# A two-block kernel on one core: VectorE's side work tied behind the step it was written beside

## The chip, the core and the metric

The kernel runs on one core of a Trainium2 chip. A core has five engines that each work through a queue of their own in order: TensorE (PE: matrix multiplies, with its weight loads shown as PEld), VectorE (DVE), ScalarE (ACT), GpSimd (POOL) and SyncE (SP, which here only starts DMAs). The metric is the device time of the whole program in microseconds (us), as the median of several runs.

## The reference

Two transformer-like blocks run one after the other on 256 tokens of 2048 channels, all in float32. The first has an attention and an mLSTM mixer and then `peer`, a layer of 16,384 one-neuron experts, which is the part that changes. The second block (two attention layers) comes after it and is not changed.

```python
def peer(h, w_query, sub_keys_1, sub_keys_2, expert_down, expert_up):
    q = (h @ w_query).reshape(B, S, 8, 256)
    s1 = einsum('bshd,nd->bshn', q[..., :128], sub_keys_1)   # 128 scores
    s2 = einsum('bshd,nd->bshn', q[..., 128:], sub_keys_2)
    v1, i1 = top_k(s1, 16);  v2, i2 = top_k(s2, 16)
    vs, pos = top_k(v1[..., :, None] + v2[..., None, :], 16) # of 16 x 16
    idx = i1[pos // 16] * 128 + i2[pos % 16];  g = softmax(vs)
    a = gelu(einsum('td,thkd->thk', x, expert_down[idx]))
    return einsum('thk,thkd->td', g * a, expert_up[idx])
```

## The kernel before

Every float32 factor of a large product is split in two numbers of fewer bits, `hi` and `lo`, so that TensorE multiplies fast (helper `load`, lines 234 to 241): SP loads a piece `raw` of 128 x 1024 weights, ScalarE writes `hi` (line 239), VectorE writes `lo = raw - hi` (line 240), and then TensorE reads both (helper `mm3w`, lines 263 and 264). `wpools` says how many buffers of `raw`, `hi` and `lo` there are; the whole program has 4, 2 and 2, and a stage can add some for itself.

For 224 of the 256 tokens the expert layer is computed densely, for all experts, and the weights of those not picked are zero.

- **Search** (`topk`): products with `w_query` and the keys, then, on VectorE alone, the top 16 of 128 and of 256 for each of 8 heads and 2 halves of the tokens (`top16`: five instructions each), and the expert numbers (`eq`, `e`). It is a generator: each `yield` hands back to the loop that drives it. It leaves `eT`, the numbers and weights of the picked experts.
- **Down** (`down(n1)`, n1 = 0 to 127): 128 experts times 224 tokens into slot n1 of `R`, from two pieces of weights with eight pairs of matmuls each. At its end ScalarE copies half of the sum (line 308), VectorE adds the other half (line 309, `joined`), and ScalarE applies gelu (line 912). `R` is three tiles: slots 0 to 63, 64 to 95, 96 to 127.
- **Picks** (`picked`, 28 calls): VectorE makes one-hot tiles `o` (lines 874 and 879), TensorE multiplies them, ScalarE and VectorE bring the result to `gst` (lines 888 and 889), and GpSimd's queue stores it to DRAM as `gd`: the dense weights of 8 tokens.
- **Weigh** (`weigh`): GpSimd loads a piece of `gd` and multiplies it into `R` (line 900); 28 calls for the first tile of `R`, 28 for the other two.
- **Up**: two passes of 1024 channels. A step takes one slot of `R`, splits it into `w` (`split`: ScalarE line 312, VectorE line 313), loads one piece of weights, and runs 16 matmuls on eight accumulators.
- **Gathered rows** (`gathered`): the last 32 tokens are not in the dense part. Their rows of `expert_down` and `expert_up` are fetched by 64 indirect DMAs of 1 MB on GpSimd's queue (line 1026, two buffers), and VectorE uses each fetched tile once (a dot product at line 1036, a sum at line 1043).

The code says in which step a gathered row, a piece of the search or a pick stands. But the order of each engine's queue is made when the kernel is built, by a scheduler that puts an instruction in as soon as it reckons that its operands and buffers are there; `load` has a head start over its neighbours (`soon`). Nothing held the side work at the place in the code where it stood. On the chip each queue then runs strictly in that order.

Of the kernel before, what the change touches and what calls it, by code (L numbers as in the profile page):

```python
# [9 lines left out]
F32 = mybir.dt.float32  # L10
# [9 lines left out]
P = 128  # L20
S = 256
# [48 lines left out]
SD = 224  # L70
# [100 lines left out]
class K:  # L171
# [134 lines left out]
    def joined(self, out, ps):  # L306

        self.nc.scalar.copy(out, ps[:, 1, :])
        self.nc.vector.tensor_add(out, ps[:, 0, :], out)  # L309

    def split(self, hi, lo, src):
        self.nc.scalar.copy(hi, src)
        self.nc.vector.tensor_sub(lo, src, hi.bitcast(F32))  # L313

    def split_g(self, hi, lo, src, gain):

# [498 lines left out]
    def peer(self, x, r, xd, x2d):  # L815
# [4 lines left out]
        mm = nc.tensor.matmul  # L820
        ctx = ExitStack()
        hT = self.xt_tiles(self.pool(ctx, "ph", 1, "right"))
        wctx = ExitStack()
        self.wpools(wctx, 1, 2, 2, "right")
        sctx = ExitStack()
        sp = self.pool(sctx, "pr", 1, "right")
        some = sp.tile([P, NK, SG], F32, name="some")
# [17 lines left out]
        def slot(n1):  # L845
            i = 0 if n1 < 64 else 1 if n1 < 96 else 2
            return R[i][:, n1 - cuts[i], :]

        def more_R():
            i = len(R)  # L850
            n = cuts[i + 1] - cuts[i]
            R.append(self.pool(rctx, "R", 1).tile([P, n, SD], F32, name=f"R{i}"))

        ep = self.pool(wctx, "pe", 1, "right")
        eT = [ep.tile([P, S], F32, name=f"eT{i}") for i in range(2)] + [ep.tile([P, S, 2], F32, name="gT")]
        gd = self.dp.tile([P, P * SD], F32, name="gd")
        top, actx = ExitStack(), ExitStack()
        self.ada_open(actx, 3)
# [33 lines left out]
        def weigh(pool, which, t0):  # L892

            n0, n = cuts[which[0]], cuts[which[-1] + 1] - cuts[which[0]]
            st = pool.tile([P, 64, 8], F32, tag="gld", name=self.nm("gld"))[:, :n]
            o = t0 * P + n0 * 8
            nc.gpsimd.dma_start(st.rearrange("p n t -> p (n t)"), gd[:, o:o + n * 8])
            for i in which:
                d = R[i][:, :, t0:t0 + 8]
                nc.gpsimd.tensor_mul(d, d, st[:, cuts[i] - n0:cuts[i + 1] - n0, :])  # L900

        def down(n1):
            ps = self.ps([P, 2, SD], "mm")
            for s in range(2):
                hi, lo = self.load(a["down"], n1 * 2048 + s * 1024, 1024)
                for i in range(8):
                    c = s * 8 + i
                    w = slice(i * P, i * P + P)
                    self.mm3w(ps, hi[:, w], lo[:, w], hT[2][:, c, :, 0:SD], c == 0, c == NK - 1)
            r = slot(n1)  # L910
            self.joined(r, ps)
            nc.scalar.activation(r, r, AF.Gelu)  # L912

        for n1 in range(32):
            down(n1)
        n0 = 32
        for _ in search:
            down(n0)
            n0 += 1
        top.close()  # L920
        gctx = ExitStack()
        gp = self.pool(gctx, "pg", 2, "right")
        for n1 in range(n0, P):
            if n1 == 64:
                more_R()
            if n1 == 96:
                gctx.close()
                wctx.close()
                lp = self.pool(ctx, "pl", LAG1, "right")
                more_R()  # L930
            if n1 < 96:
                for i in range((n1 - n0) * (SD // 8) // (96 - n0), (n1 + 1 - n0) * (SD // 8) // (96 - n0)):
                    picked(i * 8)
            down(n1)
            if n1 >= 96 and n1 - 96 < SD // 8:
                weigh(lp, (0,), (n1 - 96) * 8)
        ctx.close()

        yctx = ExitStack()
# [9 lines left out]
        for i, (c0, c1) in enumerate(UP_PASSES):  # L949
            nb = (c1 - c0) // P  # L950
            acc = [self.ps([P, 2, SD], "at" if b < 4 else "mm") for b in range(nb)]
            for n1 in range(P):
                if i == 0 and n1 == 64:
                    lctx.close()
                hi, lo = self.load(a["up"], off, 1024)
                off += 1024
                w = up.tile([P, 2, SD], F32R, tag="w", name=self.nm("w"))
                self.split(w[:, 0, :], w[:, 1, :], slot(n1))
                for b in range(nb):
                    cs = slice(b * P, b * P + P)  # L960
                    self.mm3w(acc[b], hi[:, cs], lo[:, cs], w, n1 == 0, n1 == P - 1)
                if i == 0 and n1 % 2 == 1 and n1 // 2 < SD // 8:
                    weigh(lp, (1, 2), n1 // 2 * 8)
                k = i * P + n1
                if (k + 1) * 66 // 248 > k * 66 // 248:
                    next(rows, None)
            for b in range(nb):
                c = c0 // P + b
                g = self.av[:, 5, c:c + 1]
                nc.scalar.activation(yT[:, c, 0:SD], acc[b][:, 1, :], AF.Copy, scale=g)  # L970
                nc.vector.scalar_tensor_tensor(yT[:, c, 0:SD], acc[b][:, 0, :], g, yT[:, c, 0:SD], op0=OP.mult, op1=OP.add)
# [84 lines left out]
    def topk(self, tp, hT, eT, idd, gwd):  # L1056
# [22 lines left out]
        for h in range(8):  # L1079
            for t in range(2):  # L1080
                v = T("v", [2, 16], bufs=2)
                for half in range(2):
                    self.top16(tp, sc[:, h, t, half, :], P, v[:, half, :], idx[:, t, half, h, :])
                cand = T("cand", [16, 16], bufs=2)
                nc.vector.tensor_add(cand, v[:, 0, :].unsqueeze(2).to_broadcast([P, 16, 16]),
                                     v[:, 1, :].unsqueeze(1).to_broadcast([P, 16, 16]))
                self.top16(tp, cand.rearrange("p a b -> p (a b)"), 256, vs[:, t, h, :], pos[:, t, h, :])
        for t in range(2):
            ts = slice(t * P, t * P + P)
            fi = T("fi", [2, 8, 16])  # L1090
            nf = T("nf", [8, 16])
            nc.vector.tensor_copy(fi, idx[:, t])
            for half in range(2):
                pi = T("pi", [8, 16], U32)
                if half == 0:
                    nc.vector.tensor_single_scalar(pi, pos[:, t], 4, op=OP.logical_shift_right)
                else:
                    nc.vector.tensor_single_scalar(pi, pos[:, t], 15, op=OP.bitwise_and)
                pf = T("pf", [8, 16])
                nc.vector.tensor_copy(pf, pi)  # L1100
                eq = T("eq", [8, 16, 16])
                e = T("e", [8, 16])
                for h in range(8):
                    q = eq[:, h, :, :]
                    nc.vector.tensor_tensor(q, pf[:, h, :].unsqueeze(2).to_broadcast([P, 16, 16]),
                                            self.iota[:, 0:16].unsqueeze(1).to_broadcast([P, 16, 16]), op=OP.is_equal)
                    nc.vector.tensor_mul(q, q, fi[:, half, h, :].unsqueeze(1).to_broadcast([P, 16, 16]))
                nc.vector.tensor_reduce(e.rearrange("p a b -> p (a b)"), eq.rearrange("p a b c -> p (a b) c"),
                                        axis=AX.X, op=OP.add)
                if t == 1 and half == 0:  # L1110
                    nc.vector.tensor_scalar(nf, e, 128.0, None, op0=OP.mult)
                elif t == 1:
                    nc.vector.tensor_add(nf, nf, e)
                    nu = T("nu", [8, 16], U32)
                    nc.vector.tensor_copy(nu, nf)
                    nc.gpsimd.dma_start(idd, nu[P - SG:].rearrange("p a b -> p (a b)"))
                yield
                nc.vector.tensor_copy(eT[half][:, ts], self.to_eT(e))
            g = T("g", [8, 16])
            nc.vector.tensor_sub(g, vs[:, t], vs[:, t, :, 0:1].to_broadcast([P, 8, 16]))  # L1120
            nc.scalar.activation(g, g, AF.Exp)
            z = T("z", [8])
            nc.vector.tensor_reduce(z, g, axis=AX.X, op=OP.add)
            nc.vector.reciprocal(z, z)
            nc.vector.tensor_mul(g, g, z.unsqueeze(2).to_broadcast([P, 8, 16]))
            if t == 1:
                nc.gpsimd.dma_start(gwd, g[P - SG:].rearrange("p a b -> p (a b)"))
            yield
            ps = self.to_eT(g)
            hi = T("ghi", [P], F32R)  # L1130
            nc.scalar.copy(hi, ps)
            nc.vector.tensor_copy(eT[2][:, ts, 0], hi.bitcast(F32))
            nc.vector.tensor_sub(eT[2][:, ts, 1], ps, hi.bitcast(F32))
# [407 lines left out]
```

## Time and profile before

| what | value |
|---|---|
| median of three runs | 3271.24 us (3266.43 to 3271.97) |
| the profiled execution | 3278.16 us, its span 3276.0 us |
| PE, DVE, ACT, POOL busy, share of the span | 90%, 71%, 48%, 8% |
| mean granted TensorE clock, share of 2.4 GHz | 0.95 |

The page's slices show three places where TensorE's digit falls under 9 for long. Two are short (slices of 82 us each); the third is the first pass of up, where four slices in a row have a 5 and a clock digit of 7. The span is cut below at the first and last `joined` of the downs and at the end of the up passes: downs from 682 to 1444, up from 1444 to 2371. A window's row tells for each engine how long it was busy in it. A row of a timeline has the start, the duration, the engine, the line and the operation, and in square brackets how long the engine had been idle and who ended it.

### The profile page before, as it was taken

The page shows a single profiled execution, that of the slowest core. Times are in us where ns is not written, and L with a number is a line of the kernel's source. Part 1 is how long each engine was busy: PE and PEld are TensorE (multiplying, and loading weights), DVE is VectorE, ACT ScalarE, POOL GpSimd, SP SyncE. Part 2 cuts the span into 40 slices and gives each one's busy share as a digit, 9 for nine tenths or more (in the row PEclk, how much of TensorE's full clock was granted, in tenths as well). Part 3 has the DMA queues.
Part 4 walks back from the last instruction along what each step waited for, and adds up shares of the span by engine and source line. Part 5 has one row for each costly group of instructions (what it writes and reads, how often), then busy time and mean ns, then how long its engine had stood idle before and what let it go on. Part 6 is the DMA issues. An engine that isn't in the chain of part 4 may idle for free. (4 is left out here: it accounts for less than half of the span.)

```text
span 3276.0 us, 43208 instructions
## 1 busy us (share of the span) xinstructions
PE 2934.5 (90%) x15738; PEld 2540.2 (78%) x15738; DVE 2310.3 (71%) x3774; ACT 1586.6 (48%) x2585; POOL 277.3 (8%) x281
## 2 busy tenths in 40 slices
PE   6899998979999998985556899989999999999998
PEld 4577887868898887884445788878878888888887
DVE  7889976997788886556666555555568885566664
ACT  4455645424454544441212345545456665566663
POOL 0020000000000005227422000000000000000000
PEclk9899999989999999997777999999999999999999
DMA  9888885835566667678777665555653446545555
GB/s 400 322 314 318 327 296 192 331 122 190 180 209 214 216 214 230 224 235 292 280 276 276 209 198 188 195 181 197 198 178 126 136 151 219 183 165 168 167 167 167
DMA packets 182299, 724.86 MB, mean 221 GB/s; under 512 B 21367, under 2 KB 22435, under 8 KB 161059
## 3 DMA queue, kind: packets, MB, share of 16 engines
q1 hardware_dynamic: 152640, 604.70, 54.0%
q0 software_dynamic: 18640, 99.44, 8.2%
q10 hardware_dynamic: 10806, 17.95, 1.7%
q8 instruction: 124, 2.03, 0.3%
q14 instruction: 89, 0.73, 0.1%
HBM read 698.64 MB, written 23.38 MB: 220 GB/s over the span
## 5 line engine op out<-in xcount | busy, mean ns | idle before, releaser
L240 DVE TENSOR_TENSOR lo<-raw,hi 128x1024 fp32r<-128x1024 f32 x962 | 1182.3, 1232 | 668.9 <-ACT hi L239 662.8
L239 ACT CAST hi<-raw 128x1024 fp32r<-128x1024 f32 x962 | 993.1, 1042 | 1049.8 <-PE ps L263 630.9
L263 PE MATMUL ps<-xT,hi 128*128 128x448 f32 (+2 forms) x3104 | 1044.5, 388 | 25.6 <-ACT hi L239 20.6
L263 PE MATMUL ps<-w,hi 128*128 128x448 f32 x2048 | 727.6, 408 | 181.8 <-DVE w L313 173.4
L264 PE MATMUL ps<-xT,lo 128*128 128x224 f32 (+2 forms) x3104 | 852.8, 275 | 38.4 <-DVE lo L240 37.3
L263 PEld LDWEIGHTS ps<-xT,hi 128*128 128x128 f32 (+1 forms) x3104 | 590.2, 190 | 104.1 <-ACT hr L323 12.0
L264 PEld LDWEIGHTS ps<-xT,lo 128*128 128x128 f32 (+1 forms) x3104 | 596.8, 192 | 56.9 <-DVE lo L240 52.9
L263 PEld LDWEIGHTS ps<-w,hi 128*128 128x128 f32 x2048 | 416.0, 203 | 257.6 <-DVE w L313 218.2
L264 PE MATMUL ps<-w,lo 128*128 128x224 f32 x2048 | 566.8, 277 | 0.0
L255 PE MATMUL ps<-hi,xT 128*128 128x512 f32 x1152 | 462.9, 403 | 15.1 <-ACT xT L449 11.7
L256 PE MATMUL ps<-lo,xT 128*128 128x512 f32 x1152 | 462.7, 402 | 1.8 <-DVE lo L240 1.4
L257 PE MATMUL ps<-hi,xT 128*128 128x512 f32 x1152 | 462.6, 402 | 0.0
L264 PEld LDWEIGHTS ps<-w,lo 128*128 128x128 f32 x2048 | 423.3, 207 | 0.0
L255 PEld LDWEIGHTS ps<-hi,xT 128*128 128x128 f32 x1152 | 221.0, 192 | 65.4 <-ACT xT L449 13.1
L256 PEld LDWEIGHTS ps<-lo,xT 128*128 128x128 f32 x1152 | 221.2, 192 | 51.9 <-DVE lo L240 4.2
L257 PEld LDWEIGHTS ps<-hi,xT 128*128 128x128 f32 x1152 | 220.3, 191 | 49.5 <-DVE xT L450 0.7
L379 DVE CUSTOM_DVE_ANT_0 aw<-aw,sB 128x2048 f32<-128x2048 f32 x96 | 220.0, 2306 | 27.5 <-ACT sB L366 19.0
L912 ACT ACTIVATE R<-R 128x224 f32<-128x224 f32 x128 | 50.1, 392 | 331.5 <-DVE R L309 331.5
L1036 DVE CUSTOM_DVE_ANT_0 rows<-rows,hB 128x2048 f32<-128x2048 f32 x32 | 73.8, 2307 | 66.7 <-DMA rows<-in_down_rows_dram,gidx 66.7
L1043 DVE SCALAR_TENSOR_TENSOR gacc<-rows,gdot,gacc 128x2048 f32<-128x2048 f32 x31 | 72.9, 2351 | 57.7 <-DMA rows<-in_up_rows_dram,gidx 57.7
L313 DVE TENSOR_TENSOR w<-R,w 128x224 fp32r<-128x224 f32 x256 | 106.5, 416 | 0.0
L900 POOL TENSOR_TENSOR R<-R,gld 128x256 f32<-128x256 f32 (+1 forms) x84 | 97.7, 1181 | 36.2 <-DMA gld<-gd 35.6
(398 smaller groups left out, 2479.1 us busy)
## 6 DMA issues: line engine op xcount, KB each, us to landing
raw<-in_down_dram SPq DMA_DIRECT2D x256, 512.0 KB, 3.5
raw<-in_up_dram SPq DMA_DIRECT2D x256, 512.0 KB, 3.3
aw<-in_w_ada_dram SPq DMA_DIRECT2D x96, 1024.0 KB, 7.7
raw<-in_b_in_dram SPq DMA_DIRECT2D x128, 512.0 KB, 3.3
raw<-in_w_in_dram SPq DMA_DIRECT2D x112, 512.0 KB, 6.1
raw<-in_a_in_dram SPq DMA_DIRECT2D x49, 512.0 KB, 3.2
raw<-in_w_out_dram SPq DMA_DIRECT2D x32, 512.0 KB, 4.0
raw<-in_w_query_dram SPq DMA_DIRECT2D x32, 512.0 KB, 7.2
```

The source lines that it names most:

```text
L239: self.nc.scalar.copy(hi[:, :n], raw)
L240: self.nc.vector.tensor_sub(lo[:, :n], raw, hi[:, :n].bitcast(F32))
L255: mm(out, lh, rh, start=start, stop=False)
L256: mm(out, lh, rl, start=False, stop=False)
L257: mm(out, ll, rh, start=False, stop=stop)
L263: mm(out, wh, x, start=start, stop=False)
L264: mm(out[:, 0, :], wl, x[:, 0, :], start=False, stop=stop)
L313: self.nc.vector.tensor_sub(lo, src, hi.bitcast(F32))
L379: nc.vector.tensor_tensor_reduce(out=w, in0=w, in1=self.sB, scale=1.0, scalar=0.0, op0=OP.mult, op1=OP.add, accum_out=out)
L900: nc.gpsimd.tensor_mul(d, d, st[:, cuts[i] - n0:cuts[i + 1] - n0, :])
L1036: nc.vector.tensor_tensor_reduce(out=t, in0=t, in1=h, scale=1.0, scalar=0.0, op0=OP.mult, op1=OP.add, accum_out=dj)
L1043: nc.vector.scalar_tensor_tensor(acc, t, dj, acc, op0=OP.mult, op1=OP.add)
```

## The change

`joined` and `split` return their VectorE instruction. The blocks that drive the search, the picks and the gathered rows are put under `tc.issue_after(...)` of it: each VectorE instruction of such a block comes later in VectorE's queue than the instruction named. It is an order in one queue; instructions of other engines in the block are not held. The search has more `yield`s and is driven one or two pieces per down from down 0 on. The picks run to row 112. Buffers: the stage up to the end of the search adds one of `raw`, `hi` and `lo` each (before: 1, 2 and 2, until row 96), so it has 3 of `hi` and `lo`, and the downs after it have 2 (before: 4). From up step 64 on there is a third `hi`. The pools of `eT` and of the picks are opened earlier.

```diff
     def joined(self, out, ps):
         self.nc.scalar.copy(out, ps[:, 1, :])
-        self.nc.vector.tensor_add(out, ps[:, 0, :], out)
+        return self.nc.vector.tensor_add(out, ps[:, 0, :], out).ins
...
+        ep = self.pool(ctx, "pe", 1, "right")
+        eT = ...
+        gp = self.pool(ctx, "pg", 2, "right")
         wctx = ExitStack()
-        self.wpools(wctx, 1, 2, 2, "right")
+        self.wpools(wctx, 1, 1, 1, "right")
...
-        for n1 in range(32):
-            down(n1)
-        n0 = 32
-        for _ in search:
-            down(n0)
+        n0, end = 0, object()
+        more = True
+        while more:
+            with tc.issue_after(down(n0)):
+                for _ in range(1 + n0 % 2):
+                    more = more and next(search, end) is not end
             n0 += 1
         top.close()
-        gctx = ExitStack()
-        gp = self.pool(gctx, "pg", 2, "right")
+        wctx.close()
+        n2 = 112
         for n1 in range(n0, P):
...
-            if n1 < 96:
-                for i in range((n1 - n0) * (SD // 8) // (96 - n0), ...):
-                    picked(i * 8)
-            down(n1)
-            if n1 >= 96 and n1 - 96 < SD // 8:
-                weigh(lp, (0,), (n1 - 96) * 8)
+            with tc.issue_after(down(n1)):
+                for i in range((n1 - n0) * (SD // 8) // (n2 - n0), ...):
+                    if n1 < n2:
+                        picked(i * 8)
+            if n1 >= 100:
+                weigh(lp, (0,), (n1 - 100) * 8)
...
                 if i == 0 and n1 == 64:
                     lctx.close()
+                    self.wpools(ctx, 0, 1, 0, "right")
...
-                self.split(w[:, 0, :], w[:, 1, :], slot(n1))
+                last = self.split(w[:, 0, :], w[:, 1, :], slot(n1))
...
                 if (k + 1) * 66 // 248 > k * 66 // 248:
-                    next(rows, None)
+                    with tc.issue_after(last):
+                        next(rows, None)
```

In the up passes VectorE's queue before, at steps 23 to 25 of the first pass: a gathered row (`rows`, `gdot`) stands in every step, one `lo` and one `w` between two of them.

```order
L1036 ISA rows_15172,gdot<-rows_15172,hB 128x2048
L1036 ISA gdot 128x1
L240 TENSOR_TENSOR lo_13899<-raw_13896,hi_13898 128x1024
L313 TENSOR_TENSOR w_13902<-R_5422,w_13902 128x224
L1036 ISA rows_15275,gdot<-rows_15275,hB 128x2048
```

And now, at steps 18 to 22 (the lines' numbers have moved by some, 1036 is 1041):

```order
L1041 ISA rows_13646,gdot<-rows_13646,hB 128x2048
L1041 ISA gdot 128x1
L240 TENSOR_TENSOR lo_13734<-raw_13731,hi_13733 128x1024
L313 TENSOR_TENSOR w_13737<-R_5425,w_13737 128x224
L240 TENSOR_TENSOR lo_13763<-raw_13760,hi_13762 128x1024
L313 TENSOR_TENSOR w_13766<-R_5425,w_13766 128x224
L240 TENSOR_TENSOR lo_13788<-raw_13785,hi_13787 128x1024
L313 TENSOR_TENSOR w_13791<-R_5425,w_13791 128x224
L240 TENSOR_TENSOR lo_13817<-raw_13814,hi_13816 128x1024
L313 TENSOR_TENSOR w_13820<-R_5425,w_13820 128x224
L1041 ISA rows_13728,gdot<-rows_13728,hB 128x2048
```

Three or four steps stand between two gathered rows. Before, the 64 of them stood behind steps 5 to 62 of 256; now they stand behind steps 5 to 241, each right behind a `w`.

GpSimd's queue in the first pass now, with three multiplications of the second half of `R` (`R_9238` and `R_11282`, weighed by `gld`) around the fifth gather:

```order
L898 DMA gld_14200<-gd 128x512
L1031 DMA rows_13646<-in_down_rows_dram,gidx 128x2048
L901 TENSOR_TENSOR R_9238<-R_9238,gld_14143 128x32x8
L901 TENSOR_TENSOR R_11282<-R_11282,gld_14143 128x32x8
L901 TENSOR_TENSOR R_9238<-R_9238,gld_14200 128x32x8
L901 TENSOR_TENSOR R_11282<-R_11282,gld_14200 128x32x8
```

Before, one gather stood behind every two loads of `gld` at most. Now the fourth, the fifth and the sixth gather have 5, 10 and 10 loads of `gld`, with some two multiplications each, between them and the gather ahead.

VectorE's queue at a pick before (`o` and `gst` are the pick's tiles; at the end of down `ps_7780` the `lo` of two more downs, `ps_7864` and `ps_7912`, have been written: the last are `lo_7916` and `lo_7938`):

```order
L240 TENSOR_TENSOR lo_7916<-raw_7913,hi_7915 128x1024
L874 TENSOR_TENSOR o_7961<-cst,eT_4530 128x512
L240 TENSOR_TENSOR lo_7938<-raw_7935,hi_7937 128x1024
L309 TENSOR_TENSOR R_5422<-ps_7780,R_5422 128x224
L889 TENSOR_TENSOR gst_7828<-ps_7836,gst_7828 128x128x2
L889 TENSOR_TENSOR gst_7828<-ps_7841,gst_7828 128x128x2
L889 TENSOR_TENSOR gst_7828<-ps_7853,gst_7828 128x128x2
L889 TENSOR_TENSOR gst_7828<-ps_7858,gst_7828 128x128x2
L879 SCALAR_TENSOR_TENSOR o_7963<-cst,eT_4529,gT 128x256 x4
L874 TENSOR_TENSOR o_7978<-cst,eT_4530 128x512
L879 SCALAR_TENSOR_TENSOR o_7980<-cst,eT_4529,gT 128x256
L240 TENSOR_TENSOR lo_8000<-raw_7997,hi_7999 128x1024
```

And now (874, 879, 889 are 875, 880, 890; at the end of down `ps_9151` the `lo` of one more down, `ps_9239`, have been written; `lo_9291` and `lo_9313` are for the down behind that):

```order
L309 TENSOR_TENSOR R_5425<-ps_9151,R_5425 128x224
L875 TENSOR_TENSOR o_9200<-cst,eT_4390 128x512
L880 SCALAR_TENSOR_TENSOR o_9202<-cst,eT_4389,gT 128x256 x4
L875 TENSOR_TENSOR o_9217<-cst,eT_4390 128x512
L890 TENSOR_TENSOR gst_9199<-ps_9207,gst_9199 128x128x2
L880 SCALAR_TENSOR_TENSOR o_9219<-cst,eT_4389,gT 128x256 x2
L240 TENSOR_TENSOR lo_9291<-raw_9288,hi_9290 128x1024
L890 TENSOR_TENSOR gst_9199<-ps_9212,gst_9199 128x128x2
L880 SCALAR_TENSOR_TENSOR o_9219<-cst,eT_4389,gT 128x256 x2
L890 TENSOR_TENSOR gst_9199<-ps_9224,gst_9199 128x128x2
L890 TENSOR_TENSOR gst_9199<-ps_9229,gst_9199 128x128x2
L240 TENSOR_TENSOR lo_9313<-raw_9310,hi_9312 128x1024
```

A pick is now whole within one down: its results are added (`gst`) in the same down in which its one-hot tiles are made, so VectorE's queue goes through TensorE and ScalarE and back between two `lo`. Nine of its instructions stand between the end of a down and the first `lo` behind it, and the store of `lo` reaches one down less far ahead than before.

## Rows read from the trace of the kernel before

**Rows 1.** Windows: from, to, length, busy time (count) per engine, granted clock, DMA share, GB/s.

```profile
682.00:969.00 287.00, 254.43 (x1502) 235.28 (x1503) 229.67 (x542) 130.18 (x212) 3.19 (x6) 0.95 0.54 175
...
1444.00:1845.00 401.00, 241.43 (x1085) 212.86 (x1086) 257.63 (x233) 89.41 (x136) 169.96 (x153) 0.77 0.77 275
...
2010.00:2371.00 361.00, 344.63 (x2070) 312.31 (x2068) 204.82 (x292) 175.42 (x269) 0.99 (x2) 0.98 0.59 192
```

**Rows 2.** Waits, window 1444:1845: who waited for whom, us, times, longest.

```profile
PE ps L263 <- DVE w L313: 161.4, 49, 10.4
```

**Rows 3.** Groups by line: names, shapes, count | busy us, mean ns | idle before, releasers.

```profile
L1036 DVE CUSTOM_DVE_ANT_0 rows<-rows,hB 128x2048 f32<-128x2048 f32 x32 | 73.8, 2307 | 66.7 <-DMA rows<-in_down_rows_dram,gidx 66.7
...
L1043 DVE SCALAR_TENSOR_TENSOR gacc<-rows,gdot,gacc 128x2048 f32<-128x2048 f32 x31 | 72.9, 2351 | 57.7 <-DMA rows<-in_up_rows_dram,gidx 57.7
```

**Rows 4.** Timeline of VectorE, 1616:1622: start, us, engine, line, names [idle before].

```profile
1616.59 2.29 DVE L1036 CUSTOM_DVE_ANT_0 rows<-rows,hB 128x2048 f32<-128x2048 f32 x1 [3.12 <-DMA rows<-in_down_rows_dram,gidx]
...
1618.81 1.22 DVE L240 TENSOR_TENSOR lo<-raw,hi 128x1024 fp32r<-128x1024 f32 x1
...
1619.94 0.38 DVE L313 TENSOR_TENSOR w<-R,w 128x224 fp32r<-128x224 f32 x1
```

**Rows 5.** Timeline, 1902:1910, an up step with no gathered row.

```profile
1902.06 1.05 ACT L239 CAST hi<-raw 128x1024 fp32r<-128x1024 f32 x1 [1.53 <-PE ps L263]
...
1907.43 1.05 ACT L239 CAST hi<-raw 128x1024 fp32r<-128x1024 f32 x1 [1.53 <-PE ps L263]
...
1908.51 1.23 DVE L240 TENSOR_TENSOR lo<-raw,hi 128x1024 fp32r<-128x1024 f32 x1 [1.33 <-ACT hi L239]
...
1909.65 0.38 DVE L313 TENSOR_TENSOR w<-R,w 128x224 fp32r<-128x224 f32 x1
```

**Rows 6.** Timeline of VectorE, ends of six downs, the first and last among them.

```profile
682.15 0.40 DVE L309 TENSOR_TENSOR R<-ps,R 128x224 f32<-128x224 f32 x1
...
836.90 0.38 DVE L309 TENSOR_TENSOR R<-ps,R 128x224 f32<-128x224 f32 x1
...
841.92 0.38 DVE L309 TENSOR_TENSOR R<-ps,R 128x224 f32<-128x224 f32 x1
...
964.64 0.38 DVE L309 TENSOR_TENSOR R<-ps,R 128x224 f32<-128x224 f32 x1
...
976.97 0.39 DVE L309 TENSOR_TENSOR R<-ps,R 128x224 f32<-128x224 f32 x1
...
1443.84 0.38 DVE L309 TENSOR_TENSOR R<-ps,R 128x224 f32<-128x224 f32 x1
```

**Rows 7.** Groups by line: VectorE's search and picks.

```profile
L1051 DVE FIND_INDEX8 idx<-v,sc 128x8 uint32<-128x128 f32 x32 | 9.5, 296 | 0.0
...
L1051 DVE FIND_INDEX8 pos<-vs,cand 128x8 uint32<-128x256 f32 x16 | 6.9, 429 | 0.0
...
L1105 DVE TENSOR_TENSOR eq<-pf,cst 128x256 f32<-128x256 f32 x32 | 12.3, 415 | 0.0
...
L874 DVE TENSOR_TENSOR o<-cst,eT 128x512 fp32r<-128x512 f32 x56 | 38.4, 685 | 0.1
...
L879 DVE SCALAR_TENSOR_TENSOR o<-cst,eT,gT 128x256 fp32r<-128x256 f32 x224 | 95.6, 479 | 0.0
...
L889 DVE TENSOR_TENSOR gst<-ps,gst 128x256 f32<-128x256 f32 x112 | 39.9, 421 | 0.0
```

**Rows 8.** Windows of line 240 alone: VectorE busy (count), granted clock, DMA share, GB/s.

```profile
1300.00:1320.00 20.00, 12.28 (x7) 1.00 0.82 266
...
1380.00:1400.00 20.00, 9.37 (x8) 1.00 0.64 207
```

**Rows 9.** Timeline of GpSimd, 1480:1502: weights multiplied into R.

```profile
1486.97 2.83 POOL L900 TENSOR_TENSOR R<-R,gld 128x256 f32<-128x256 f32 x4 [1.63 <-DMA gld<-gd]
...
1493.72 3.04 POOL L900 TENSOR_TENSOR R<-R,gld 128x256 f32<-128x256 f32 x4
```

**Rows 10.** Tile rows: the gathers' DMAs.

```profile
DMA to landing us min/median/max: 5.4/7.1/10.2
```

More of the change, by code (lines that the diff above doesn't have):

```diff
@@ L308, in joined @@
         self.nc.scalar.copy(out, ps[:, 1, :])
-        self.nc.vector.tensor_add(out, ps[:, 0, :], out)
+        return self.nc.vector.tensor_add(out, ps[:, 0, :], out).ins
     def split(self, hi, lo, src):
         self.nc.scalar.copy(hi, src)
-        self.nc.vector.tensor_sub(lo, src, hi.bitcast(F32))
+        return self.nc.vector.tensor_sub(lo, src, hi.bitcast(F32)).ins
     def split_g(self, hi, lo, src, gain):
@@ L822, in peer @@
         hT = self.xt_tiles(self.pool(ctx, "ph", 1, "right"))
+        ep = self.pool(ctx, "pe", 1, "right")
+        eT = [ep.tile([P, S], F32, name=f"eT{i}") for i in range(2)] + [ep.tile([P, S, 2], F32, name="gT")]
+        gp = self.pool(ctx, "pg", 2, "right")
         wctx = ExitStack()
-        self.wpools(wctx, 1, 2, 2, "right")
+        self.wpools(wctx, 1, 1, 1, "right")
         sctx = ExitStack()
@@ L852, in more_R @@
             R.append(self.pool(rctx, "R", 1).tile([P, n, SD], F32, name=f"R{i}"))
-        ep = self.pool(wctx, "pe", 1, "right")
-        eT = [ep.tile([P, S], F32, name=f"eT{i}") for i in range(2)] + [ep.tile([P, S, 2], F32, name="gT")]
         gd = self.dp.tile([P, P * SD], F32, name="gd")
@@ L910, in down @@
             r = slot(n1)
-            self.joined(r, ps)
+            last = self.joined(r, ps)
             nc.scalar.activation(r, r, AF.Gelu)
-        for n1 in range(32):
-            down(n1)
-        n0 = 32
-        for _ in search:
-            down(n0)
+            return last
+        n0, end = 0, object()
[4 more added lines that the diff above has]
+                    more = more and next(search, end) is not end
             n0 += 1
         top.close()
-        gctx = ExitStack()
-        gp = self.pool(gctx, "pg", 2, "right")
+        wctx.close()
+        n2 = 112
         for n1 in range(n0, P):
@@ L926, in peer @@
             if n1 == 96:
-                gctx.close()
-                wctx.close()
+                more_R()
+            if n1 == 100:
                 lp = self.pool(ctx, "pl", LAG1, "right")
-                more_R()
-            if n1 < 96:
-                for i in range((n1 - n0) * (SD // 8) // (96 - n0), (n1 + 1 - n0) * (SD // 8) // (96 - n0)):
-                    picked(i * 8)
-            down(n1)
-            if n1 >= 96 and n1 - 96 < SD // 8:
-                weigh(lp, (0,), (n1 - 96) * 8)
+            with tc.issue_after(down(n1)):
+                for i in range((n1 - n0) * (SD // 8) // (n2 - n0), (n1 + 1 - n0) * (SD // 8) // (n2 - n0)):
+                    if n1 < n2:
+                        picked(i * 8)
+            if n1 >= 100:
+                weigh(lp, (0,), (n1 - 100) * 8)
         ctx.close()
@@ L1083, in topk @@
                     self.top16(tp, sc[:, h, t, half, :], P, v[:, half, :], idx[:, t, half, h, :])
+                    yield
                 cand = T("cand", [16, 16], bufs=2)
@@ L1087, in topk @@
                 self.top16(tp, cand.rearrange("p a b -> p (a b)"), 256, vs[:, t, h, :], pos[:, t, h, :])
+                yield
         for t in range(2):
@@ L1107, in topk @@
                     nc.vector.tensor_mul(q, q, fi[:, half, h, :].unsqueeze(1).to_broadcast([P, 16, 16]))
+                    if h % 2:
+                        yield
                 nc.vector.tensor_reduce(e.rearrange("p a b -> p (a b)"), eq.rearrange("p a b c -> p (a b) c"),
```

## The prediction

> **What bounds the kernel now.** I read the page's slices first, then the windows, the waits of the worst window, the groups by line, and the timelines of a slow and a clean step. TensorE is the engine to keep fed: it is busy 90% of the span. The windows show where it isn't. From 1444 to 1845, in the first pass of up, it is busy for 241 of 401 us, at a granted clock of 0.77, so part of the time at the lower of its two levels (1.2 and 2.4 GHz); in the second pass (2010 to 2371) it is busy for 345 of 361 at 0.98 [rows 1]. In the slow window TensorE waits for VectorE's `w`: 161 us in 49 waits [rows 2]. VectorE isn't short of time there (258 of 401 busy); it stands at the head of its own queue and waits for gathered rows: 66.7 and 57.7 us [rows 3]. The timeline shows how: a row waits 3.1 us for its DMA, takes 2.3, and only then come the `lo` and `w` that TensorE needs [rows 4].
>
> The downs from 682.2 to 1443.8 [rows 6] have a second loss. At 837 a down takes 5.01 us, which for 16 pairs of matmuls is TensorE's own pace; 128 of them would be 641 us, and they take 762. One part is the search, which the scheduler poured into VectorE's queue in one piece around 682 to 760; from 682 to 969 VectorE is busy 230 of 287 us and the clock is 0.95 [rows 1]. Another is the picks: two downs with a pick take 12.33 us instead of 10.03 [rows 6].
>
> **The search, spread.** Its VectorE instructions stay the same in number: five per top-16, 32 sets like the first row and 16 sets like the second (five and a sum), 5 x 9.5 + 6 x 6.9 = 89 us [rows 7]. Over the 32 downs that now carry them that is 2.8 us per down, beside 2 x 1.23 for `lo` and 0.38 for line 309, 5.6 by the rows; back to back they overlap by some 0.09 each (the `w` of [rows 4] starts 1.13 us after a `lo` of 1.22), which leaves about 4.9, just under TensorE's 5.01. The `lo` run a piece ahead with 3 buffers, so I take 32 x 5.01 = 160 us, hidden behind TensorE. The rest, 64 `eq` instructions (2 x 12.3 us [rows 7]) with as much again in sums and small ones (an estimate), is some 3 us per down over 15 downs: 5.5 us each, VectorE being now the slower, 83 us. If the cover fails, the cost is at most the whole of it, 89 + 44 us.
>
> **The picks.** They get dearer. The downs behind the search lose two `hi` and two `lo` buffers. With two, the `lo` of a down's second half can't be made before the half two back is done: `hi` 1.05, `lo` 1.23 against a half of 2.5 us. Now a pick stands in front of it. From the end of a down at 0: `hi` to 1.05, `lo` to 2.3, line 309 to 2.6, the first one-hot tiles (0.69 and 0.48 each [rows 7]) from 2.6 to 4.9. TensorE reaches the pick's first matmul in its queue at 1.9 and gets its operands at 3.7; the last of four at 4.9, so its first half ends at 5.3 instead of 2.5. The second half needs the other tiles, behind a `gst` addition that waits for ScalarE: 6.3 for the third pair of pick matmuls' first, and, since a `lo` of 1.23 stands in between, 8.6 for the last; it ends at 9.75. A down with a pick so takes 9.75, one without 5.04 to 5.2. 28 x 9.75 + 52 x 5.1 = 538 us. Bounds: as in the row of before, 12.33 - 5.01 = 7.3 per pick down (69 us less); fully in series, TensorE's 6 us, the pick's 6.2 ((38.4 + 95.6 + 39.9) / 28) and a `hi`, `lo` and `w`, 2.6: 14.8 (141 us more). I take my walk, as it follows the new queues.
>
> **Weighing beside picks.** 28 multiplications of GpSimd now run while VectorE is pressed. A `lo` took 1.75 us (12.28 / 7) in a window with them and 1.17 without [rows 8]. I charge 10 us in the downs and 5 in up. In the same rows the granted clock is 1.00, so it isn't TensorE's. The Trainium skill, page "SBUF — State Buffer", section "SBUF: two separate sides", says that VectorE with two inputs in SBUF and a GpSimd operation that reads SBUF shut each other out for a whole instruction; the trace shows a slowing by half, not a wait of the whole; by the rule the charge is 82 us, a rival below.
>
> **Downs:** 160 + 83 + 538 + 10 = 791 us, 29 more than the 762 of before.
>
> **Up, base.** Two clean steps take 5.37 us (1902.06 to 1907.43): with two buffers, ScalarE's `hi`, VectorE's `lo` and `w` follow each other [rows 5]. 64 steps x 2.68 = 172. From step 64 on there is a third `hi`, so `lo` starts as soon as its own buffer is free: 1.23 + 0.38 us against a step's 8 pairs of 2.51. 192 x 2.51 = 482 us. If the third buffer doesn't help: 33 more.
>
> **Up, gathered rows.** 64 x 2.33 us on VectorE [rows 3]. In the first 64 steps a row holds `lo` back by 1.3 us behind a step whose slack is nothing; the next step, which would have waited 0.35, doesn't: 1.0 each, 17 us for 17. Later only the part beyond the slack is late, 0.6 each, 28 us for 47. The DMA wait goes: a gather is issued when the row two before it is used, 7.5 steps or 19 us ahead, and lands in 7.1 (10.2 at most) [rows 10]. Two gathers fall out: GpSimd's queue puts ten weighings ahead of the fifth and ten more ahead of the sixth. Two weighings and a gather took 6.75 us (1486.97 to 1493.72 [rows 9]), so ten without gathers some 27. By that the fifth lands some 13 us after VectorE wants it and the sixth some 18 after, and VectorE stands in front of all `lo`: 33 us with TensorE's restart. Between 0 (if the weighing were far quicker) and 50. The very first row waits in both kernels: 4. What the second pass has beyond 128 x 2.68 = 343 of its 361 us [rows 1], the change of passes and the positions' block, stays: 18.
>
> **Up:** 172 + 482 + 17 + 28 + 33 + 4 + 18 + 5 = 759, against 2371 - 1444 = 927. A gain of 168.
>
> **Sum.** 168 - 29 = 139 us less than the profiled execution's 3278: 3139. The runs' median lies 7 us below that execution, so I forecast 3132. All queues behind up read as before, so nothing is won or lost there.
>
> **Rivals.**
>
> - *The ties put engines in series* (slower). Place: downs 0 to 112. VectorE's tied piece starts only behind line 309, which waits for TensorE; TensorE waits for the `lo` behind the piece. If nothing overlaps, the search costs its whole 133 us where the forecast has 8, 125 more, and the picks take 14.8 per down, 141 more: 3398. It decides from somewhat over half of these 266 us, where the 139 are eaten. For it: fewer buffers, and the pick's way through three engines and back. Against: with 3 buffers `lo` is a piece ahead in the search.
> - *The gathers still wait for their DMAs* as they did, 124 us in sum [rows 3]: about 3240. For it: the indirect DMA goes through a queue full of weighings. Against: 38 of the 64 come after the weighings, with 19 us of lead.
> - *All hidden.* A pick costs as before and GpSimd's queue is no brake: 69 + 33 less, 3030.
> - *The lock.* Each weighing shuts VectorE out for its whole length: 56 x 0.73 us (3.0 / 4 [rows 9]) and 28 of twice that, 82 instead of 15: 3199.
>
> **How the numbers follow.** Forecast 0.60, all hidden 0.12, lock 0.12, DMA waits 0.07, series 0.09. The forecast's own bounds (33 for the third buffer, 50 and 0 for the two gathers, 69 of the picks) give 3060 to 3200. The range goes from 3055 to 3220, which leaves out the series, the DMA waits and the far end of all hidden. Faster by over 0.2% (about what a measurement here can tell from no change): 0.89, within it 0.03, slower 0.08, which is the series where it goes past the middle.
>
> **What would show it.** Right: TensorE waits on `w` of a few tens of us instead of 161; up 760 us long with two single waits of 10 to 20 us for a gathered row within its first 120 us; downs longer than before, with some 4 us of TensorE's waiting for `o` and `lo` at each pick; no stretch in which VectorE is full at the downs' start. Wrong: downs as short as before or shorter, up steps of 2.7 us to the end, or DVE waiting for a row's DMA through both passes.

## The result and the profile after

The changed kernel takes 3175.86 us (median of four runs, 3173.10 to 3177.91) against 3271.60 for the kernel before in the same comparison: a ratio of 0.9705, interval 0.9686 to 0.9725. That is 96 us faster, inside the forecast's range and on its side, but 44 us short of the 3132 that was forecast. The profiled execution took 3177.91 us, its span 3176.2.

Cut at the same instructions, the two profiled executions (spans 3276.0 and 3176.2) compare like this:

| stretch, us | before | after | change | forecast change |
|---|---|---|---|---|
| start to the first `joined` of the downs | 671.7 | 668.7 | -3 | 0 |
| first to last `joined` | 772.1 | 825.2 | +53 | +29 |
| last `joined` to the last `w` of up | 919.8 | 767.9 | -152 | -168 |
| from there to the end | 912.4 | 914.4 | +2 | 0 |

One row has to be put right first. The end of a down at 682.15 in [rows 6] is the second, not the first. The first stands here, in VectorE's timeline of the kernel before:

```profile
671.74 0.39 DVE L309 TENSOR_TENSOR R<-ps,R 128x224 f32<-128x224 f32 x1
```

So the downs of before took 772 us from the first end to the last. These are 127 downs, as many as the forecast adds up (32, 15 and 80); the 762 that it set against them are for one less.

The page's slices of the changed kernel (busy tenths, 79 us each): where the first pass of up had 5, 5, 5 and 6 for TensorE, a 6 and a 7 are left in slices 20 and 21; the row of 8s from slice 13 to 18, in the downs, is new.

```profile
PE   6899998999998888889678999989999999999998
```

The windows of the changed kernel, cut at its own steps (columns as in [rows 1]): the downs with the search, the downs with picks, the first 64 steps of up, and the rest of up.

```profile
668.73:843.22 174.49, 166.25 (x1037) 154.59 (x1036) 168.60 (x498) 82.72 (x129) 0.00 (x0) 1.00 0.58 191
...
926.76:1415.99 489.23, 408.27 (x2312) 361.44 (x2311) 359.16 (x591) 217.16 (x373) 69.19 (x82) 0.94 0.55 184
...
1494.19:1737.74 243.55, 180.45 (x1019) 163.19 (x1020) 143.17 (x162) 84.95 (x128) 95.57 (x107) 0.88 0.70 247
1737.74:2261.80 524.06, 494.05 (x3056) 458.58 (x3056) 405.94 (x482) 258.92 (x397) 75.72 (x48) 0.99 0.80 286
```

The loss in the downs sits in the second row: TensorE works 408 of 489 us there, at a granted clock of 0.94. What is left of the old loss in up sits in the third: 180 of 244 us, clock 0.88.

In the waits from 1494 to 1845, TensorE's wait for `w` answers to [rows 2], 69 us for 161, and the second row is new in kind: three waits, of which one lasts 18.9 us.

```profile
PE ps L263 <- DVE w L313: 69.0, 33, 19.4
...
DVE rows L1041 <- DMA rows<-in_down_rows_dram,gidx: 37.2, 3, 18.9
```

The groups of gathered rows answer to [rows 3]: the work is the same, of 124 us of waiting 37 are left, all of it in the first half.

```profile
L1041 DVE CUSTOM_DVE_ANT_0 rows<-rows,hB 128x2048 f32<-128x2048 f32 x32 | 73.7, 2302 | 37.2 <-DMA rows<-in_down_rows_dram,gidx 37.2
L1048 DVE SCALAR_TENSOR_TENSOR gacc<-rows,gdot,gacc 128x2048 f32<-128x2048 f32 x31 | 72.7, 2345 | 0.0
```

In the later part of the first pass, VectorE's `w` come like this (1753.67 to 1764 has four steps). A step without a row takes 2.51 us, the one behind a row is late, and the steps behind it catch up part of it:

```profile
1753.67 0.39 DVE L313 TENSOR_TENSOR w<-R,w 128x224 fp32r<-128x224 f32 x1
...
1756.18 0.39 DVE L313 TENSOR_TENSOR w<-R,w 128x224 fp32r<-128x224 f32 x1
1756.48 2.29 DVE L1041 CUSTOM_DVE_ANT_0 rows<-rows,hB 128x2048 f32<-128x2048 f32 x1
...
1759.83 0.39 DVE L313 TENSOR_TENSOR w<-R,w 128x224 fp32r<-128x224 f32 x1
...
1761.27 0.39 DVE L313 TENSOR_TENSOR w<-R,w 128x224 fp32r<-128x224 f32 x1
...
1764.34 0.39 DVE L313 TENSOR_TENSOR w<-R,w 128x224 fp32r<-128x224 f32 x1
```

### The profile page after: what moved, and what is told of

Same layout as the page of the kernel before. It is cut to its first block, busy times and chain, and to the rows that moved or that the text cites. A ratio compares the mean times of both kernels' runs of the same rounds, so it can differ in the third digit from the quotient of the medians.

```text
span 3176.2 us, 43138 instructions
## 1 busy us (share of the span) xinstructions
PE 2888.3 (91%) x15738; PEld 2504.3 (79%) x15738; DVE 2336.5 (74%) x3774; ACT 1605.2 (51%) x2585; POOL 279.8 (9%) x281
## 5 line engine op out<-in xcount | busy, mean ns | idle before, releaser
L263 PE MATMUL ps<-xT,hi 128*128 128x448 f32 (+2 forms) x3104 | 1056.2, 389 | 16.2 <-ACT hi L239 10.5
L263 PE MATMUL ps<-w,hi 128*128 128x448 f32 x2048 | 669.5, 384 | 95.6 <-DVE w L313 92.9
L264 PE MATMUL ps<-w,lo 128*128 128x224 f32 x2048 | 546.7, 267 | 0.0
L263 PEld LDWEIGHTS ps<-w,hi 128*128 128x128 f32 x2048 | 391.4, 191 | 148.8 <-DVE w L313 113.3
L264 PEld LDWEIGHTS ps<-w,lo 128*128 128x128 f32 x2048 | 398.0, 194 | 0.0
L886 PE MATMUL ps<-o,o 128*128 128x256 f32 x224 | 79.8, 361 | 78.7 <-DVE o L880 78.3
L886 PEld LDWEIGHTS ps<-o,o 128*128 128x128 f32 x224 | 49.3, 220 | 103.2 <-issue 90.8
L889 ACT COPY gst<-ps 128x256 f32<-128x256 f32 x112 | 45.6, 407 | 122.5 <-PE ps L886 122.5
```

Source lines behind the costliest of these rows:

```text
L263: mm(out, wh, x, start=start, stop=False)
L264: mm(out[:, 0, :], wl, x[:, 0, :], start=False, stop=stop)
L886: mm(ps[:, k, :], o2[:, i + k, :], o1[:, i + k].rearrange("p a n -> p (a n)"), start=True, stop=True)
```

## The experiments

All are made from the changed kernel (3176 us), but the first, which starts from the kernel before. "Downs" and "up" are cut as above, each from one profiled execution. A ratio is to the kernel before, which ran beside each set; its median was 3269 to 3275 us from set to set, so differences between medians of two sets are good to some 6 us.

**The gathered rows' tie alone** (from the kernel before; `split` returns its instruction as in the change):

```diff
-                    next(rows, None)
+                    with tc.issue_after(last):
+                        next(rows, None)
```

> The kernel before with one edit: the gathered rows are tied behind the split of the step they are written in. Theory (the pile of gathered rows is what held up the first pass): downs stay as in the kernel before (772 us between the first and the last line 309 of R), up becomes as in the changed kernel plus the third hi's part, 768 + 33 = 800 us from the first w to the last instead of 920; the two long waits for a gathered row of 18 and 20 us stay, since GpSimd's queue reads the same as in the changed kernel. Time 3150. Rival (the gain of up comes from the third hi and the new buffers): up stays at 920 or loses at most 30, time 3240 to 3270.

Measured: 3159.4 us, ratio 0.9648 (0.9627 to 0.9669). Downs 771.4, up 807.5, and the two waits stay (steps of 20.7 and 20.6 us). This one edit gives more than the whole change, 115 us by its ratio; the other parts of the change together cost some 16 to 19. The windows, first 64 steps and the rest:

```profile
1440.97:1681.80 240.83, 177.94 (x1024) 160.66 (x1024) 143.99 (x163) 84.51 (x128) 99.15 (x108) 0.90 0.70 249
1681.80:2248.18 566.38, 509.10 (x3055) 460.16 (x3056) 400.67 (x482) 258.42 (x397) 76.86 (x48) 0.99 0.72 265
```

The first row is like that of the changed kernel (243.55). The second is 42 us longer than its 524.06.

**Without the third `hi`:**

```diff
                     lctx.close()
-                    self.wpools(ctx, 0, 1, 0, "right")
```

> The changed kernel without the third hi from up step 64. Theory: steps without a gathered row go back from 2.51 to 2.68 us and a row costs 1.0 instead of 0.6 us; the 192 steps from step 64 take 33 to 50 us more, time 3209 to 3225. Rival (TensorE is fed by lo's own buffers, the third hi is idle): no change, 3176.

Measured: 3212.5 us, ratio 0.9814 (0.9792 to 0.9836), 37 more. The steps from 64 on take what they take in the experiment before:

```profile
1731.13:2297.88 566.75, 510.67 (x3055) 461.58 (x3056) 400.65 (x481) 258.30 (x397) 76.75 (x48) 0.99 0.71 265
```

So the third buffer is worth 43 us in this stretch, inside the 33 to 50 of the theory.

**Free picks** (the tie on the picks taken away, buffers as in the changed kernel):

```diff
-            with tc.issue_after(down(n1)):
-                for i in range(...):
-                    if n1 < n2:
-                        picked(i * 8)
+            down(n1)
+            for i in range(...):
+                if n1 < n2:
+                    picked(i * 8)
```

> The changed kernel without the tie on the picks: they are written behind their down as before, and the scheduler places them. Buffers stay at two hi and two lo. Theory 1 (the tie makes a pick a way through three engines inside one down): a pick costs 2.3 to 3.5 us beyond its down instead of 5.5, 28 of them 60 to 90 us less, time 3086 to 3116. Theory 2 (the two lost buffers of hi and lo are what makes it dear): at most 10 us less, 3166 to 3176.

Measured: 3106.4 us, ratio 0.9492 (0.9474 to 0.9509), 70 less than the changed kernel. The 80 downs from the 47th on take 499.6 us instead of 567.1. What TensorE waits for changes with it. In the changed kernel, from 926.76 to 1415.99, it is the one-hot tiles (for `lo` it waits once, 1.2 us):

```profile
PE ps L886 <- DVE o L880: 78.3, 62, 2.6
```

With free picks, from 927.24 to 1405, TensorE has no wait for `o` left, and `lo` takes its place with less:

```profile
PE ps L264 <- DVE lo L240: 49.8, 28, 3.0
```

The scheduler makes the tiles a down ahead and adds the results a down behind, so the way through three engines spans two downs.

**Free picks and four `hi` and `lo` until row 96:**

```diff
-        n2 = 112
+        n2 = 96
+        wctx = ExitStack()
+        self.wpools(wctx, 1, 2, 2, "right")
...
             if n1 == 96:
+                wctx.close()
                 more_R()
```

> The changed kernel without the tie on the picks and with four hi and four lo until row 96, where the picks then end. Both theories on the picks: a pick costs what it cost in the kernel before, 2.3 us beyond its down; the downs from the 47th on take 28 x 2.3 + 80 x 5.05 = 468 instead of 567 us, time 3077. If only this one and not the kernel with free picks alone is faster, the buffers were it. Rival (the picks are dear because they now run beside GpSimd's weighing): most of the 99 us stays, over 3140.

Measured: 3102.6 us, ratio 0.9488 (0.9467 to 0.9509). That can't be told from the experiment before. The 80 downs take 492.0 us, not the 468 expected; in the kernel before they take 474.5. Where the 17 us between them lie stays open.

**The four buffers alone, picks tied:** the edit above without the one on the picks.

> The changed kernel, picks tied as in it, but with four hi and four lo until row 96, where the picks then end. The free picks took 67 us off the downs with two buffers and 75 with four. Theory (the tie alone makes the pick dear): the 80 downs from the 47th on stay within 20 us of the 567, time 3156 to 3176. Rival (either remedy does, since four buffers let the lo of a whole down be there before the pick): 490 to 520 us, time 3100 to 3130.

Measured: 3172.8 us, ratio 0.9702 (0.9667 to 0.9738), no different from the changed kernel. The 80 downs take 561.9 us. That sum alone doesn't settle it, because two things in it work against each other: almost no weighing runs beside the picks here (worth 21 us, see below), and where the buffers change at row 96 three downs take 33.7 us, where some 20 would be usual. The single down does settle it. From one end to the next, a down with a pick takes 9.93 us, as with two buffers:

```profile
1188.54 0.39 DVE L309 TENSOR_TENSOR R<-ps,R 128x224 f32<-128x224 f32 x1
...
1198.47 0.39 DVE L309 TENSOR_TENSOR R<-ps,R 128x224 f32<-128x224 f32 x1
```

With the two experiments before: the tie alone made the picks dear, and two more buffers do nothing for a tied pick.

**Without the tie on the search:**

```diff
-            with tc.issue_after(down(n0)):
-                for _ in range(1 + n0 % 2):
-                    more = more and next(search, end) is not end
+            down(n0)
+            for _ in range(1 + n0 % 2):
+                more = more and next(search, end) is not end
```

> The changed kernel without the tie on the search's pieces: the scheduler pours them into VectorE's queue at the first ten downs, as before. Theory: the 47 downs from the first on take 298 us as in the kernel before instead of 258, time 3216. Rival (VectorE has the same work in these 47 downs either way, so the order is worth nothing): 258 us, 3176.

Measured: 3200.1 us, ratio 0.9781 (0.9751 to 0.9811), 24 more, not the 40 of the theory. The windows of the first 47 downs, untied and (second fence) in the changed kernel:

```profile
672.21:955.50 283.29, 249.81 (x1492) 231.62 (x1493) 211.24 (x515) 126.56 (x195) 1.00 (x2) 0.96 0.50 171
```

```profile
668.73:926.76 258.03, 242.67 (x1506) 225.66 (x1505) 243.21 (x636) 126.44 (x196) 1.00 (x2) 0.99 0.58 188
```

Tied, VectorE has 32 us more work inside these downs (untied, part of the search runs ahead of the first `joined`) and is nearly full, 243 of 258 us; the stretch is still 25 us shorter.

**Weighings tied behind the gathers**, in GpSimd's queue (`got` is the gather issued last):

```diff
-                    weigh(lp, (1, 2), n1 // 2 * 8)
+                    with tc.issue_after(self.got):
+                        weigh(lp, (1, 2), n1 // 2 * 8)
```

> The changed kernel with the weighing of the second half of R tied, in GpSimd's queue, behind the gather that was issued last, so that no gather stands behind ten weighings. Theory: the two waits of 18 and 20 us for a gathered row go, the first 64 steps of up take 205 instead of 244 us, time 3138. Rival 1 (the gathers are late by their DMAs, not by the weighings): waits stay, 3176. Rival 2 (the weighings now come too late for step 64): a new wait there of 10 to 40 us, 3150 to 3180.

Measured: 3166.6 us, ratio 0.967 (0.9634 to 0.9705), an interval that meets that of the changed kernel. The two long waits are gone, but the first 64 steps take 233.7 us, not 205. That is no clear gain over the 243.5 of the changed kernel: in seven other executions that leave these steps as they are (the rows' tie alone, no third `hi`, and the five with another order of picks or search or less weighing in the downs), they take 235.0 to 245.1. Four rows of GpSimd's timeline show what came in their place:

```profile
1590.47 1.04 POOL L1032 DMA_INDIRECT rows<-in_down_rows_dram,gidx  x1 [0.16 <-issue]
1591.50 1.12 POOL L898 DMA_DIRECT2D gld<-gd  x2
1598.83 6.58 POOL L901 TENSOR_TENSOR R<-R,gld 128x256 f32<-128x256 f32 x4 [6.21 <-DMA gld<-gd]
1605.57 1.04 POOL L1032 DMA_INDIRECT rows<-in_down_rows_dram,gidx  x1 [0.15 <-issue]
```

The loads now start only behind a gather, GpSimd waits 6.2 us for them, multiplies for 6.6, and only then issues the next gather: 15.1 us from one to the next, where VectorE wants one each 3.75 steps, some 10 us.

**Without the weighing of the first tile of `R`:**

```diff
-            if n1 >= 100:
-                weigh(lp, (0,), (n1 - 100) * 8)
```

> The changed kernel without the weighing of the first 64 slots of R: 28 loads and 28 multiplications of GpSimd are left out, so the output lacks these weights. Theory (GpSimd slows VectorE beside it): the 17 picks that took 11.0 us go back to the 9.93 of the others, the downs from the 47th to the last take 20 us less than 567, time 3154. Rival (the second tile of R or the shorter lead of the later picks makes them slower, not GpSimd): 567 us stay, 3176. By a lock for the whole length of each multiplication: 28 x 1.4 = 39 us less, 3137.

Measured: 3153.3 us, ratio 0.9633 (0.9601 to 0.9664), 23 less; the 80 downs take 545.7 us, 21 less. VectorE's one-hot tiles in the changed kernel (first fence) and here:

```profile
L880 DVE SCALAR_TENSOR_TENSOR o<-cst,eT,gT 128x256 fp32r<-128x256 f32 x224 | 103.4, 511 | 0.0
...
L875 DVE TENSOR_TENSOR o<-cst,eT 128x512 fp32r<-128x512 f32 x56 | 48.0, 857 | 0.0
```

```profile
L880 DVE SCALAR_TENSOR_TENSOR o<-cst,eT,gT 128x256 fp32r<-128x256 f32 x224 | 95.7, 480 | 0.0
L875 DVE TENSOR_TENSOR o<-cst,eT 128x512 fp32r<-128x512 f32 x56 | 38.3, 684 | 0.0
```

Without GpSimd beside them they have the durations of [rows 7] again: VectorE works 17 us less on them, of the 21 that the downs gain.

**Gathered rows from up step 58 on**, one each third step, when the weighing is over:

```diff
-                if (k + 1) * 66 // 248 > k * 66 // 248:
+                if k >= 56 and (k - 55) * 66 // 192 > (k - 56) * 66 // 192:
```

> The changed kernel with the gathered rows starting at up step 58 instead of step 3, one every third step, when the weighing of the second half of R is through. Theory (the two waits of 18 and 20 us come from weighings ahead of the gathers in GpSimd's queue, and tying the weighings behind the gathers only put their loads' 5 to 6 us in the gathers' way): the first 64 steps of up take 172 for their two-buffer pace and 10 to 20 for the weighing beside them, 185 to 190 instead of 244; the other steps carry 17 rows more at 0.6 each, 534 instead of 524. Time 3176 - 45 = 3131. Rival (one row every third step is too dense for two buffers and the DMAs): 30 us or more come back behind step 64, 3160 to 3180.

Measured: 3136.1 us, ratio 0.960 (0.9573 to 0.9627), 40 less. Its windows, and its group of line 1041, which no longer waits at all:

```profile
1495.13:1684.73 189.60, 173.51 (x1015) 153.63 (x1016) 125.78 (x132) 84.93 (x128) 77.70 (x92) 0.99 0.69 239
1684.73:2220.77 536.04, 500.91 (x3060) 461.87 (x3060) 436.64 (x511) 259.05 (x397) 99.32 (x62) 0.99 0.82 308
```

```profile
L1041 DVE CUSTOM_DVE_ANT_0 rows<-rows,hB 128x2048 f32<-128x2048 f32 x32 | 73.1, 2285 | 0.0
```

**Without the weighing in up** (slots 64 to 127 of `R`):

```diff
-                if i == 0 and n1 % 2 == 1 and n1 // 2 < SD // 8:
-                    weigh(lp, (1, 2), n1 // 2 * 8)
```

> The changed kernel without the weighing of slots 64 to 127 of R: 28 loads and 56 multiplications of GpSimd in the first pass of up are left out, so the output lacks these weights. Theory: nothing stands ahead of the gathers, the two long waits go, and VectorE has no company: the first 64 steps take 172 + 17 + 5 = 194 to 205 us instead of 244, one time 3127 to 3137. Rival (the waits are the gathers' own): 235 to 244 us stay, 3176.

Measured in one run: 3134.9 us. The first 64 steps take 195.9 us, with the 17 gathered rows in them, and no step is longer than 7.4 us. So it was the weighings ahead of the gathers, not the gathers, that made the long waits; the rest of the gain is not split between them and the company that GpSimd keeps VectorE.

**The best of it:** free picks, four buffers until row 96, late rows.

> The changed kernel with free picks, four hi and four lo until row 96, and the gathered rows from step 58 on. If the parts add up: 3102.6 of the kernel with free picks and buffers, less the 45 of the late rows: 3058. Rival (the late rows give nothing when up begins earlier): 3100.

Measured: 3061.8 us (five runs, 3059.9 to 3063.9), ratio 0.9373 (0.9354 to 0.9391), 114 less than the changed kernel. The parts add up. Its slices:

```profile
PE   6899999899998999999999999899999999999998
```

## Why the prediction was right, and where its size was off

The direction and the main gain were right, for the reason given: the gathered rows at the head of VectorE's queue were the loss in up. The first experiment shows it with one edit. 44 us are missing. The table has 39 of them, 24 in the downs, 16 in up and 1 the other way elsewhere; the other 5 are the step from the profiled execution to the median, which was 7 us before and is 2 now. In the stretches they come from four terms of the sum.

- **The search, 32 x 5.01 = 160: measured 174.5.** VectorE doesn't stay under TensorE's pace; two downs take 10.84 us. It is busy for 168.6 of the 174.5 us, so the sign "no stretch in which VectorE is full at the downs' start" did not come true. The step that failed is the overlap of 0.09 us taken for each instruction. In VectorE's timeline of one piece in the changed kernel, there is no such overlap where an instruction uses the result of the one ahead of it: the second maximum starts 0.31 us after the start of a replacement of 0.28, and the loading row behind the first maximum starts 0.32 after that maximum's start, which takes 0.28. Behind the search for an index, whose result the replacement doesn't use, there is an overlap of 0.09. Also, each search for an index or replacement has a loading row of 0.07 to 0.09 us ahead of it, which the sum left out:

```profile
691.62 0.28 DVE L1055 MAX8 v<-sc 128x8 f32<-128x128 f32 x1
691.94 0.09 DVE L1056 MATCH_VALUE_LOAD idx<-v,sc 128x8 f32 x1
692.02 0.29 DVE L1056 FIND_INDEX8 idx<-v,sc 128x8 uint32<-128x128 f32 x1
692.22 0.07 DVE L1057 MATCH_VALUE_LOAD t<-v,sc 128x8 f32 x1
692.28 0.28 DVE L1057 MATCH_REPLACE8 t<-v,sc 128x128 f32<-128x128 f32 x1
692.59 0.29 DVE L1058 MAX8 v<-t 128x8 f32<-128x128 f32 x1
```

  The tail of 15 downs was 83 forecast and 83.5 measured. That is the sum only: its single downs take 4.06 to 9.19 us, not 5.5 each, and half of the term was an estimate, so the agreement may be luck.
- **A pick, 9.75: measured 9.93** where GpSimd doesn't disturb it. The walk held step by step. VectorE's and TensorE's timelines from one end of a down to the next: the wait for `o` (forecast 1.8, here 1.55), the late `lo`, the end.

```profile
1008.21 0.38 DVE L309 TENSOR_TENSOR R<-ps,R 128x224 f32<-128x224 f32 x1
1008.51 0.68 DVE L875 TENSOR_TENSOR o<-cst,eT 128x512 fp32r<-128x512 f32 x1
1009.73 0.36 PE L886 MATMUL ps<-o,o 128*128 128x256 f32 x1 [1.55 <-DVE o L880]
1011.40 0.60 PE L263 MATMUL ps<-xT,hi 128*128 128x448 f32 x1
1012.42 1.22 DVE L240 TENSOR_TENSOR lo<-raw,hi 128x1024 fp32r<-128x1024 f32 x1
1016.99 1.23 DVE L240 TENSOR_TENSOR lo<-raw,hi 128x1024 fp32r<-128x1024 f32 x1 [0.89 <-ACT hi L239]
1018.14 0.39 DVE L309 TENSOR_TENSOR R<-ps,R 128x224 f32<-128x224 f32 x1
```

  The walk left out that behind its wait TensorE runs some matmuls at 0.60 us instead of 0.37. The granted clock is 0.50 there, between 1011.2 and 1014.0, which is the lower of its two levels. It cost nothing here: of the two downs with a pick below, each from end to end, the first has the full clock throughout, and both take 9.93 us.

```profile
993.26:1003.19 9.93, 7.36 (x43) 6.40 (x44) 8.46 (x18) 4.29 (x8) 0.54 (x1) 1.00 0.39 140
1008.21:1018.14 9.93, 8.41 (x43) 7.76 (x44) 8.46 (x19) 4.24 (x8) 0.53 (x1) 0.83 0.45 158
```

  The cause given for the dear pick, fewer buffers and the pick in one piece within a down, was half right: with the picks tied, four buffers changed nothing.
- **Weighing beside picks, 10: measured 21.** The price per weighing was taken too low, and the rival that priced it at its whole length had the mechanism (below). 17 of the 28 downs with a pick take 11.15 us on average, the other 11 take 9.95.
- **Up, first 64 steps: forecast 172 + 17 + 33 + 4 + 5 = 231, measured 243.5.** The two gathers behind ten weighings each were foreseen, place and cause: the steps take 20.7 and 23.2 us, 38 in sum beyond a step's 2.68, for 33. Here are the fourth and the fifth gather in GpSimd's timeline of the changed kernel, 35 us apart where the forecast had 27 for ten weighings, and the fifth row, for which VectorE waits:

```profile
1533.68 1.03 POOL L1031 DMA_INDIRECT rows<-in_down_rows_dram,gidx  x1
...
1568.71 1.01 POOL L1031 DMA_INDIRECT rows<-in_down_rows_dram,gidx  x1 [0.30 <-issue]
```

```profile
1575.13 2.29 DVE L1041 CUSTOM_DVE_ANT_0 rows<-rows,hB 128x2048 f32<-128x2048 f32 x1 [16.41 <-DMA rows<-in_down_rows_dram,gidx]
```

  The weighing beside the steps was charged 5 us. The kernel with late rows has no row until step 58 and takes 189.6 for these 64 steps, 17.6 beyond 172: 4.1 are up's second step (6.76 us, in which ScalarE's `hi` waits 4.33 for TensorE; the step is long in every run, and the sum had left it out), 3.6 are the steps from 58 on, and some 10 are left for the weighing.
- **Up, from step 64: forecast 482 + 28 + 18 = 528**, to the end of the window some 7 us behind the last `w`; measured 524.1 to the last `w`. A clean step of 2.51 and the 0.6 for a row hold.

The 34 us that the downs' terms came short (14.5 in the search, 0.5 in its tail, 19 in the 80 downs behind it) show as 24 in the table, since the base was read 10 us too short, at the wrong end of a down. The two errors partly cancel, which is luck. The bounds that the forecast names don't add up to its "3060 to 3200": taken together from 3132 they give 3030 to 3182. Nothing of the rival "the gathers still wait" came true after the weighings; nor of "series": that one needed over half of 266 us, and the downs took 34 more than their terms.

The parts of the change by the experiments' ratios: the tie on the rows is worth 115 us, the third `hi` 36, the tie on the search 25, and the tie on the picks costs 70. The sum, 106, is near the 96 measured; it need not meet it, since the first was measured from the kernel before and the others by taking a part out of the changed one.

## What to carry to other kernels

Tie side work behind a step's own work where it waits for something slow, a DMA above all, since what waits at the head of a queue stops all behind it. Don't tie a chain that goes through several engines and back into one step: left free, it stretches over two and costs less. A transfer issued from an engine's queue is only as early as the work ahead of it there, so read the issuing engine's queue as well; starting its users later was worth some 35 to 40 us here, while tying the other work behind the transfers showed no clear gain.

## What the runs showed of the hardware

A multiplication on GpSimd and an instruction on VectorE that reads two tiles from SBUF (the on-chip memory that holds all tiles but the sums of matmuls, `ps`) exclude each other for what is left of the one that came first. In the changed kernel's timeline:

```profile
1078.61 1.25 POOL L901 TENSOR_TENSOR R<-R,gld 128x512 f32<-128x512 f32 x1 [2.98 <-DMA gld<-gd]
1078.68 1.73 DVE L875 TENSOR_TENSOR o<-cst,eT 128x512 fp32r<-128x512 f32 x1
```

The one-hot tile starts 0.07 us after the multiplication and takes 1.73 us where it took 0.68 at 1008.51: 1.05 more, ending 0.55 after the multiplication's end. Ten of the 56 took over 1.4 us. The other way round, a multiplication that starts 0.21 us behind a `lo` takes 2.18 us instead of 1.25:

```profile
1232.96 1.23 DVE L240 TENSOR_TENSOR lo<-raw,hi 128x1024 fp32r<-128x1024 f32 x1 [1.40 <-ACT hi L239]
1233.17 2.18 POOL L901 TENSOR_TENSOR R<-R,gld 128x512 f32<-128x512 f32 x1 [3.66 <-DMA gld<-gd]
```

An instruction that reads one of its two tiles from `ps` isn't held: line 309 at 1062.45, 0.04 us behind the start of a multiplication, took its usual 0.38.

The meeting with the pick is no accident: the store of the pick before was issued at 1071.63, and through two DMAs the weighing follows 7 us behind it, just when the next pick begins. The prediction had read a slowing by half from a mean; in that window of the kernel before, single `lo` took 1.22, 1.87 and 1.91 us, struck not at all or for what was left of a multiplication. The Trainium skill, page "SBUF — State Buffer", section "SBUF: two separate sides", says that whichever of the two starts first has the shared port for its whole instruction, and the trace agrees, with the 1.05 us above. The prediction's charge by the length of each multiplication was still too high: 41 of its 82 us were for the 28 in the downs, and leaving these out gave 21 us back, 0.77 each. Some come second, like the one above, or strike an instruction that isn't late; how the rest divides was not followed.
